# First stage of a transformer block: the w_ada sums on column groups of TensorE in place of VectorE

## The chip, the cores and the metric

The kernel runs on one core of one Trainium2 chip. The metric is the device time of one execution, in microseconds (us). Before the change three runs took 434.02 to 434.26 us, with a median of 434.11.

## The reference, cut to what matters

The block takes 256 tokens `x` of width 1024 and one conditioning vector `c`. Its first stage is this:

```
c_act = silu(c)
mod   = c_act @ w_ada + b_ada                  # 1024 x 6144; six parts of 1024
sh_m, sc_m, gt_m, sh_f, sc_f, gt_f = split(mod, 6)
h     = rms_norm(x, g_mix) * (1 + sc_m) + sh_m
proj  = h @ w_in                               # q, k, v of two attentions, and gates
```

Two attentions, a gated mix, and a feed-forward part with a short convolution follow; the change doesn't touch them. All inputs are fp32.

## The kernel before, in words

Each weight product is made of three fp32r products: a high part (`hh`, `wh`, a rounded copy made by ScalarE) and a low part (`hl`, `wl`, the difference): hh·wh, hl·wh and hh·wl.

The first stage is a loop (L510) over the eight row blocks j of w_in, which are also the eight column blocks of the normed and modulated `h`. It is emitted in a fixed order: every engine runs its instructions as they stand in the code. Step j has these parts:

- `products` (L403): 24 matmuls `pA` of 256 moving columns into four PSUM banks (q and k) and 6 matmuls `pV` of 512 columns (v).
- For step j+1, ahead of the products of j: two transposes of x (L390) into a bank `h`, and the sums of the shift and scale columns of block j+1, that is c_act times 1024 rows of w_ada for 128 columns of each. Part of the eight row blocks k is summed on VectorE: `ada_mac` (L383, L385) multiplies each block by its element of c and adds up in `acc`; the list `KV` sets how many. The rest goes to TensorE in `sums` (L396), where a 128x128 block of w_ada is stationary and one column of c moves. `acc_sums` (L401) adds up `acc` over the partitions with a column of ones.
- `w_hi` (L478): ScalarE makes `whA` (1024 wide) and `whB` (512). It stands ahead of `modulated` in the code.
- `modulated`: VectorE makes `ab` (two columns, L441 and L443), ScalarE makes `hf` from the transposed x (L445) and `hh` (L446).
- `h_lo` (L492) and `w_lo` (L486): `hl`, `wlA` on VectorE and `wlB` on GpSimd; from step 2 on `hl` is GpSimd's too.
- `load_on`: the loads of w_ada block j+3 and w_in block j+2, on SyncE's queue, three slots for each.

Ahead of the loop c is read and passed through silu, TensorE runs 24 warm-up matmuls (L115), and `norm1` (L315) forms each token tile's root mean square: a square with a running sum on ScalarE (`sq`), `ms` on VectorE, a power on GpSimd, and the scaling of the first 256 columns of x on VectorE (L320). The other 768 columns follow in step 0 (L516). GpSimd also builds a table of biases (`rrow`, `rdram`), which comes back as `toep`.

Of the kernel before, what the change touches and what calls it, by code (L numbers as in the profile page):

```python
# [53 lines left out]
def block_kernel(ctx: ExitStack, tc: tile.TileContext, x, c, w_ada, b_ada, g_mix, w_in, w_br_moba,  # L54
# [53 lines left out]
    nc.vector.tensor_mul(ca, ce, cps[:, :KT])  # L108

# [237 lines left out]
    toep = att.tile([P, NH, S], F32, tag="gb", name="toep")  # L347
# [3 lines left out]
    M = [8, 0, 0, 0, 0, 0, 0, 0]  # L351
    KV, KV0 = [4, 4, 5, 6, 7, 7, 7, 7], [5, 4]
# [16 lines left out]
    def win_load(j):
        raw = raw_tile(f"wA{j}")  # L370
        nc.sync.dma_start(raw[:, :1536], w_in[j * P:(j + 1) * P, QA:QA + 1536])
        return raw

    def kv(j, i):
        return KV0[i] if j == 0 else KV[j]

    def ada_mac(j, wk, acc=None, parts=slice(0, 2)):
        if acc is None:
            acc = small.tile([P, 2, P], F32, tag="acc0", name=f"acc0_{j}")
        a = acc[:, parts, :]  # L380
        for k in range(kv(j, parts.start)):
            if k == 0:
                nc.vector.tensor_scalar(a, wk[:, parts, 0, :], ca[:, 0:1], None, op0=ALU.mult)  # L383
            else:
                nc.vector.scalar_tensor_tensor(a, wk[:, parts, k, :], ca[:, k:k + 1], a, op0=ALU.mult, op1=ALU.add)  # L385
        return acc

    def transposes(j, ps, ts=range(NT)):
        for t in ts:
            nc.tensor.transpose(ps[:, t * P:(t + 1) * P], xs[t][:, j * P:(j + 1) * P], ident)  # L390

    def sums(j, ps, wk):

        for i in range(2):
            for k in range(kv(j, i), KT):
                nc.tensor.matmul(ps[:, S + i:S + i + 1], wk[:, i, k, :], ca[:, k:k + 1],  # L396
                                 start=i == 0 and k == kv(j, 0), stop=False)

    def acc_sums(j, ps, acc, parts=(0, 1)):
        for i in parts:  # L400
            nc.tensor.matmul(ps[:, S + i:S + i + 1], acc[:, i, :], ones[:, 0:1], start=False, stop=i == 1)  # L401
# [47 lines left out]
    wks = {0: ada_load(0)}  # L449
    vr = const.tile([108, P], F32, name="vr")  # L450
# [5 lines left out]
    wws = {0: win_load(0)}  # L456
    for j in (1, 2):
        wks[j] = ada_load(j)
    wws[1] = win_load(1)
    r1 = [norm1(0)]  # L460
    acc0 = ada_mac(0, wks[0], parts=slice(0, 1))
    r1.append(norm1(1))
    ada_mac(0, wks[0], acc0, slice(1, 2))
# [6 lines left out]
    gmix, gffn, bconv = vc[:, 48:56], vc[:, 56:64], vc[:, 64:108]  # L470

# [9 lines left out]
    def w_lo(j, wh):  # L481

        wl = wlp.tile([P, 1024], F32R, tag="wl", name=f"wlA{j}"), wlp.tile([P, 1024], F32R, tag="wl", name=f"wlB{j}")

        def piece(eng, i, a, n):
            eng.tensor_sub(wl[i][:, a:a + n], wws[j][:, i * 1024 + a:i * 1024 + a + n], wh[i][:, a:a + n].bitcast(F32))  # L486

        piece(nc.gpsimd, 1, 0, 512)
        return [(wh[i], wl[i]) for i in range(2)], [lambda: piece(nc.vector, 0, 0, 1024)]

    def h_lo(j, hf):
        (nc.gpsimd if j > 1 else nc.vector).tensor_sub(hl[:, j, :], hf, hh[:, j, :].bitcast(F32))  # L492

    def load_on(j):
        if j + 3 < KT:
            wks[j + 3] = ada_load(j + 3)
        if j + 2 < KT:
            wws[j + 2] = win_load(j + 2)

    ps = bank(sm, "h1_0")  # L500
    transposes(0, ps)
    sums(0, ps, wks[0])
    acc_sums(0, ps, acc0, (0,))
    acc_sums(0, ps, acc0, (1,))
    warm_up(8)
    wh = w_hi(0)
    next(wh)
    hf = modulated(0, ps)
    wh = list(wh)[-1]
    for j in range(KT):  # L510
        if j + 1 < KT:
            acc = ada_mac(j + 1, wks[j + 1])
        h_lo(j, hf)
        wp, fill = w_lo(j, wh)
        if j == 0:
            fill += [lambda t=t: nc.vector.tensor_scalar(xs[t][:, S:], xs[t][:, S:], r1[t], None, op0=ALU.mult)  # L516
                     for t in range(NT)]
        for f in fill:
            f()
# [270 lines left out]
    def pairs_put(p0):  # L790
        def put(t, ps):
            if p0 not in tb:
                tb[p0] = (att.tile([P, KT, S], F32R, tag="gb", name="qk01") if p0 == 0
                          else slot("h2h", [P, KT, S], F32R, "qk23"))
# [220 lines left out]
    wcr = [slot("trif", [88, P], F32, "wcr0"), slot("wcr1", [44, P], F32, "wcr1")]  # L1015
# [52 lines left out]
```

## Time and profile before

| | |
|---|---|
| median of three runs | 434.11 us |
| the profiled execution | 434.69 us, span 433.0 us |
| TensorE matmul / weight load busy | 410.1 us (95%) / 364.4 us (84%) |
| VectorE, ScalarE, GpSimd busy | 335.6 (77%), 254.0 (59%), 41.4 us (10%) |
| mean granted TensorE clock | 0.982 of full speed |
| moved by DMA | 94.44 MB, mean 218 GB/s |

The span is what the profiler saw from the first to the last instruction, and times in rows count from its start. A busy share is an average over stages of different kinds; the stage of the change is the first 67 us. In the timeline rows a piece begins at the first number and lasts the second; matmuls overlap in the pipeline, so the distance from one start to the next, not the duration, is what one costs in a row of many. An fp32 matmul shows as two instructions.

### The profile page before, as it was taken

To read this page: it belongs to the slowest core of one execution; us is meant where nothing else is said; L and a number is where in the kernel's file an instruction comes from. 1 tells how busy PE (TensorE), PEld (TensorE's weight loads), DVE (VectorE), ACT (ScalarE), POOL (GpSimd) and SP (SyncE) were. 2 spreads that over 40 slices of the span, in tenths; PEclk is the share of its full clock that TensorE was granted. 3 is DMA by queue.
4 is the path that set the end of the run, shared out by engine and by line. 5 is a ranking of instruction groups with operands and counts; after the bars stand their busy time and mean duration, and the time that the engine had idled before them with its cause. 6 is when DMAs were issued, how large, how long until landed. Compare 5 with 4: busy or idle time off the path is not lost.

```text
span 433.0 us, 6769 instructions
## 1 busy us (share of the span) xinstructions
PE 410.1 (95%) x2598; PEld 364.4 (84%) x2598; DVE 335.6 (77%) x509; ACT 254.0 (59%) x397; POOL 41.4 (10%) x76
## 2 busy tenths in 40 slices
PE   7899889999799899999996999999999999999993
PEld 7898887789698688788884899999999999888882
DVE  3789969689689977996858779999998888546333
ACT  3244537867966779942446758666776666433312
POOL 3624430000001010000041000000000000000001
PEclk9999969999999999999999999999999999999997
DMA  8999987988467556577537487677576655473102
GB/s 260 323 325 332 290 287 259 323 292 289 147 239 254 188 203 234 197 244 288 177 115 242 155 277 251 202 254 247 178 226 175 183 193 195 149 266 122 47 0 97
DMA packets 67128, 94.44 MB, mean 218 GB/s; under 512 B 2558, under 2 KB 45697, under 8 KB 67096
## 3 DMA queue, kind: packets, MB, share of 16 engines
q1 hardware_dynamic: 65943, 90.77, 63.6%
q0 software_dynamic: 576, 1.67, 1.2%
q10 hardware_dynamic: 576, 1.57, 1.0%
q8 instruction: 20, 0.33, 0.3%
q14 instruction: 13, 0.10, 0.1%
HBM read 92.94 MB, written 1.06 MB: 217 GB/s over the span
## 4 chain that ended last, share of the span: by engine, by line
PE 61%; DVE 13%; ACT 9%; DMA 8%; issue 4%; SPq 1%; POOL 1%; POOLq 0%; DVEq 0%; ACTq 0%
PE ps_up L252 26%; PE ps_down L164 14%; DVE acc L385 4%; PE ps_out L164 4%; DMA ada_gtm<-in_w_ada_dram 3%; PE ps_yb L164 3%; PE ps_ya L164 3%; PE ps_qkb L252 3%; DMA raw_wA<-in_w_in_dram 2%; PE ps_up L164 2%; DMA ada<-in_w_ada_dram 2%; PE pA L406 1%; DMA ada_shf<-in_w_ada_dram 1%; DVE wl_gate L139 1%; SPq L365 1%
## 5 line engine op out<-in xcount | busy, mean ns | idle before, releaser
L138 ACT CAST wh_up<-raw_up 128x1024 fp32r<-128x1024 f32 x44 | 46.1, 1050 | 27.7 <-PE ps_up L252 21.9
L252 PE MATMUL ps_up<-h2h__2313,wh_up 128*128 128x256 f32 x320 | 58.0, 283 | 0.0
L252 PE MATMUL ps_up<-h2h__2313,wl_up 128*128 128x256 f32 x320 | 57.9, 283 | 0.0
L139 DVE TENSOR_TENSOR wl_up<-raw_up,wh_up 128x1024 fp32r<-128x1024 f32 x42 | 51.1, 1220 | 8.5 <-ACT wh_up L138 8.3
L252 PE MATMUL ps_up<-h2l__2314,wh_up 128*128 128x256 f32 x320 | 57.1, 279 | 0.0
L252 PEld LDWEIGHTS ps_up<-h2h__2313,wl_up 128*128 128x128 f32 x320 | 46.9, 191 | 0.0
L139 DVE TENSOR_TENSOR wl_down<-raw_down,wh_down 128x1024 fp32r<-128x1024 f32 x22 | 26.9, 1224 | 25.6 <-ACT wh_down L138 25.6
L252 PEld LDWEIGHTS ps_up<-h2l__2314,wh_up 128*128 128x128 f32 x320 | 46.6, 190 | 0.0
L252 PEld LDWEIGHTS ps_up<-h2h__2313,wh_up 128*128 128x128 f32 x320 | 46.4, 189 | 0.2
L138 ACT CAST wh_down<-raw_down 128x1024 fp32r<-128x1024 f32 x22 | 23.2, 1053 | 32.2 <-PE ps_down L164 23.6
L941 DVE SCALAR_TENSOR_TENSOR cv<-ps_up,wc,cv 128x255 f32<-128x255 f32 (+1 forms) x80 | 34.4, 476 | 1.4 <-ACT cv L935 0.9
L164 PE MATMUL ps_down<-wl_down,hh_a 128*128 128x512 f32 x88 | 34.9, 397 | 0.0
L164 PE MATMUL ps_down<-wh_down,hh_a 128*128 128x512 f32 x88 | 34.7, 395 | 0.0
L164 PE MATMUL ps_down<-wh_down,hl_a 128*128 128x512 f32 x88 | 34.7, 394 | 0.0
L164 PE MATMUL ps_gate<-wh_gate,hh 128*128 128x512 f32 x64 | 26.2, 409 | 1.9 <-DVE vbl L145 1.5
L385 DVE SCALAR_TENSOR_TENSOR acc<-ada,ca,acc 128x256 f32<-128x256 f32 (+1 forms) x43 | 24.7, 576 | 1.5
L164 PE MATMUL ps_gate<-wl_gate,hh 128*128 128x512 f32 x64 | 25.4, 396 | 0.0
L164 PE MATMUL ps_gate<-wh_gate,hl 128*128 128x512 f32 x64 | 25.3, 396 | 0.0
L935 ACT ACTIVATE cv<-ps_up,vc,wc 128x256 f32<-128x256 f32 x40 | 20.5, 562 | 5.7 <-PE ps_up L252 5.7
L139 DVE TENSOR_TENSOR wl_gate<-raw_gate,wh_gate 128x1024 fp32r<-128x1024 f32 x16 | 20.3, 1286 | 3.2 <-ACT wh_gate L138 3.2
L478 ACT CAST whA<-raw_wA 128x1024 fp32r<-128x1024 f32 (+1 forms) x9 | 8.6, 958 | 22.9 <-DMA raw_wA<-in_w_in_dram 22.9
L164 PEld LDWEIGHTS ps_down<-wh_down,hh_a 128*128 128x128 f32 x88 | 16.5, 188 | 4.1
(268 smaller groups left out, 930.7 us busy)
## 6 DMA issues: line engine op xcount, KB each, us to landing
raw_up<-in_w_up_dram SPq DMA_DIRECT2D x44, 512.0 KB, 5.0
raw_down<-in_w_down_dram SPq DMA_DIRECT2D x10, 1024.0 KB, 5.0
ada<-in_w_ada_dram SPq DMA_DIRECT2D x16, 512.0 KB, 7.5
raw_gate<-in_w_in_dram SPq DMA_DIRECT2D x8, 1024.0 KB, 7.2
raw_wA<-in_w_in_dram SPq DMA_DIRECT2D x8, 768.0 KB, 9.0
raw_qkb<-in_w_in_dram SPq DMA_DIRECT2D x8, 512.0 KB, 5.7
ada_gtm<-in_w_ada_dram SPq DMA_DIRECT2D x8, 512.0 KB, 5.4
ada_shf<-in_w_ada_dram SPq DMA_DIRECT2D x8, 512.0 KB, 5.7
```

The lines of the kernel that those rows point to most:

```text
L138: nc.scalar.copy(wh[:, :n], t[:, a:a + n])
L139: (lo or nc.vector).tensor_sub(wl[:, :n], t[:, a:a + n], wh[:, :n].bitcast(F32))
L164: nc.tensor.matmul(ps, sx(k)[:, sl], w[:, c0:c0 + n], start=first and i == 0, stop=last and i == 2)
L252: nc.tensor.matmul(st.ps[f // 2][:, f % 2 * S:(f % 2 + 1) * S], wi[:, kk * 512 + f * P:kk * 512 + (f + 1) * P], sx(k0 + kk), start=first a ...
L365: nc.sync.dma_start(raw[:, i * D:(i + 1) * D].rearrange("p (k f) -> p k f", f=P), w_ada[:, i * D + j * P:i * D + (j + 1) * P].rearrange("( ...
L385: nc.vector.scalar_tensor_tensor(a, wk[:, parts, k, :], ca[:, k:k + 1], a, op0=ALU.mult, op1=ALU.add)
L406: nc.tensor.matmul(psqk[f // 2][:, f % 2 * S:(f % 2 + 1) * S], wp[0][n == 2][:, f * P:(f + 1) * P], (hh, hl, hh)[n][:, j, :], start=j == 0 ...
L478: nc.scalar.copy(wh[i][:, a:a + n], wws[j][:, i * 1024 + a:i * 1024 + a + n])
L935: nc.scalar.activation(ct[:, b, :], tp[:, b * S:(b + 1) * S], AF.Identity, bias=bconv[:, fb:fb + 1], scale=wc[:, 88 + fb:89 + fb])
L941: nc.vector.scalar_tensor_tensor(ct[:, b, d:], tp[:, b * S:(b + 1) * S - d], wc[:, (2 - d) * 44 + fb:(2 - d) * 44 + fb + 1], ct[:, b, d:], ...
```

## The change

Per step, all eight row blocks of the w_ada sums go to TensorE with the roles changed: a 128x32 tile `cw` with one column of c in its first column (the other 31 are zero) is stationary, and 256 columns of w_ada (128 of the shift, 128 of the scale) move. Block k writes to the 32 PSUM partitions that begin at 32·(k mod 4), so four column groups of the array are used, each twice. VectorE copies the 128x256 result to `row`, and two matmuls with a column of ones turn it into two columns. x is scaled in full and transposed ahead of the loop into a tile `xT`. `ab` goes from VectorE to ScalarE, `hl` and `wlB` from GpSimd to VectorE. w_ada has four slots of its own in a pool that is closed behind the stage, and two loads more are issued ahead of the loop.

```diff
+    cw = const.tile([P, KT, 32], F32, name="cw")
+    nc.vector.memset(cw, 0.0)
+    nc.vector.tensor_copy(cw[:, :, 0], ca)
...
     def norm1(t):
         sq = slot(f"xn{t}", [P, D], F32, f"sq{t}")
         ss = small.tile([P, 1], F32, tag="ss1", name=f"ss1_{t}")
         nc.scalar.activation(sq, xs[t], AF.Square, accum_out=ss)
         r = rstd_of(ss, f"n1_{t}")
-        nc.vector.tensor_scalar(xs[t][:, :S], xs[t][:, :S], r, None, op0=ALU.mult)
-        return r
+        for half in range(2):
+            sl = slice(half * 512, (half + 1) * 512)
+            nc.vector.tensor_scalar(xs[t][:, sl], xs[t][:, sl], r, None, op0=ALU.mult)
+        for half in range(2):
+            tp = bank(sm, f"xt{t}{half}")
+            for a in range(4):
+                j = 4 * half + a
+                nc.tensor.transpose(tp[:, a * P:(a + 1) * P], xs[t][:, j * P:(j + 1) * P], ident)
+            nc.scalar.copy(xT[:, 4 * half:4 * half + 4, t * P:(t + 1) * P], tp.rearrange("p (a b) -> p a b", a=4))
...
-    M = [8, 0, 0, 0, 0, 0, 0, 0]
-    KV, KV0 = [4, 4, 5, 6, 7, 7, 7, 7], [5, 4]
+    M1, M2 = 4, 12
...
+    def row_sums(j):
+        cs = bank(sm, f"cs_{j}")
+        for k in range(KT):
+            g = slice(k % 4 * 32, k % 4 * 32 + 32)
+            nc.tensor.matmul(cs[g, 0:S].rearrange("p (i f) -> p i f", i=2), cw[:, k, :], ads[j][:, :, k, :],
+                             start=k < 4, stop=k >= 4)
+        row = small.tile([P, S], F32, tag="acc0", name=f"row_{j}")
+        nc.vector.tensor_copy(row, cs[:, 0:S])
+        return row
+
+    def column_sums(j, row):
+        ps = bank(sm, f"h1_{j}")
         for i in range(2):
+            nc.tensor.matmul(ps[:, i:i + 1], row[:, i * P:(i + 1) * P], ones[:, 0:1], start=i == 0, stop=i == 1)
+        return ps
...
     def modulated(j, ps):
-        nc.vector.tensor_scalar(ab[:, 0:1], ps[:, S + 1:S + 2], b1[:, 8 + j:9 + j], gmix[:, j:j + 1],
-                                op0=ALU.add, op1=ALU.mult)
-        nc.vector.tensor_scalar(ab[:, 1:2], ps[:, S:S + 1], vc[:, j:j + 1], None, op0=ALU.add)
+        nc.scalar.activation(ab[:, 0:1], ps[:, 1:2], AF.Identity, bias=bg[:, j:j + 1], scale=gmix[:, j:j + 1])
+        nc.scalar.activation(ab[:, 1:2], ps[:, 0:1], AF.Identity, bias=vc[:, j:j + 1])
-        nc.scalar.activation(hf, ps[:, :S], AF.Identity, bias=ab[:, 1:2], scale=ab[:, 0:1])
+        nc.scalar.activation(hf, xT[:, j, :], AF.Identity, bias=ab[:, 1:2], scale=ab[:, 0:1])
...
     for j in range(KT):
         todo = products(j, wp)
         if j + 1 < KT:
-            run(todo, M[j])
-            transposes(j + 1, ps)
-            sums(j + 1, ps, wks[j + 1])
-            acc_sums(j + 1, ps, acc)
+            run(todo, M1)
+            row = row_sums(j + 1)
+            run(todo, M2)
+            hf = modulated(j + 1, column_sums(j + 1, row))
+            h_lo(j + 1, hf)
             wh = list(w_hi(j + 1))[-1]
-            hf = modulated(j + 1, ps)
+            wp = w_lo(j + 1, wh)
         run(todo)
```

TensorE before, where the products of step 2 have ended; `h_4` is the bank of block 4, `ada` its part of w_ada, `pA` the q and k banks with the products of step 3, `pV` those of v:

```order
L390 MATMUL h_4_486<-ident,x_94 128x128
L390 MATMUL h_4_486<-ident,x_96 128x128
L396 MATMUL h_4_486<-ca,ada_402 128x1 x2
L401 MATMUL h_4_486<-ones,acc_4_473 128x1 x2
L406 MATMUL pA_146<-hh,whA_428 128x256 x2
L406 MATMUL pA_147<-hh,whA_428 128x256 x2
L406 MATMUL pA_148<-hh,whA_428 128x256 x2
L406 MATMUL pA_149<-hh,whA_428 128x256 x2
L411 MATMUL pV_150<-whB_429,hh 128x512
```

TensorE now, at the start of the products of step 3; `cs` is the bank of the row sums of block 4:

```order
L405 MATMUL pA_150<-hh,whA_469 128x256 x2
L405 MATMUL pA_151<-hh,whA_469 128x256 x2
L390 MATMUL cs_500<-ada_363,cw 32x256 x8
L405 MATMUL pA_152<-hh,whA_469 128x256 x2
L405 MATMUL pA_153<-hh,whA_469 128x256 x2
L410 MATMUL pV_154<-whB_470,hh 128x512
L410 MATMUL pV_155<-whB_470,hh 128x512
L405 MATMUL pA_150<-hl,whA_469 128x256 x2
L405 MATMUL pA_151<-hl,whA_469 128x256 x2
L405 MATMUL pA_152<-hl,whA_469 128x256 x2
L399 MATMUL h_4_523<-ones,row_509 128x1 x2
L405 MATMUL pA_153<-hl,whA_469 128x256 x2
```

The transposes and one-column matmuls that stood between two steps are gone; the row sums stand behind four products of step 3, and the column sums (`h_4`) come 12 products later, with 14 behind them.

ScalarE before, from the squares of x to the first step's casts:

```order
L318 ACTIVATE sq_172,ss_0_173<-x_94 128x1024
L318 ACTIVATE sq_186,ss_1_187<-x_96 128x1024
L467 COPY vc<-vps 128x108
L478 CAST whA_259<-raw_wA_162 128x512
L445 ACTIVATE hf_265<-h_0_239,ab_262 128x256
L446 CAST hh<-hf_265 128x256
L478 CAST whA_259<-raw_wA_162 128x512
L478 CAST whB_260<-raw_wA_162 128x512
```

ScalarE now, the same place; `xt` are banks of transposed x:

```order
L326 ACTIVATE sq_181,ss_0_182<-x_95 128x1024
L336 COPY xT<-xt_190 128x4x128
L336 COPY xT<-xt_196 128x4x128
L326 ACTIVATE sq_202,ss_1_203<-x_97 128x1024
L336 COPY xT<-xt_211 128x4x128
L336 COPY xT<-xt_217 128x4x128
L464 COPY vc<-vps 128x108
L440 ACTIVATE ab_284<-h_0_281,bg,vc 128x1
L441 ACTIVATE ab_284<-h_0_281,vc 128x1
L443 ACTIVATE hf_287<-xT,ab_284 128x256
L444 CAST hh<-hf_287 128x256
```

The square of the second token tile (`sq`) stood right behind the first; now two copies out of the transposes' banks stand between them, and four copies ahead of `ab` and `hf` of step 0.

ScalarE before, for step 3 in the loop:

```order
L478 CAST whA_428<-raw_wA_405 128x1024
L478 CAST whB_429<-raw_wA_405 128x512
L445 ACTIVATE hf_435<-h_3_419,ab_432 128x256
L446 CAST hh<-hf_435 128x256
```

ScalarE now, for step 3:

```order
L440 ACTIVATE ab_462<-h_3_459,bg,vc 128x1
L441 ACTIVATE ab_462<-h_3_459,vc 128x1
L443 ACTIVATE hf_465<-xT,ab_462 128x256
L444 CAST hh<-hf_465 128x256
L477 CAST whA_469<-raw_wA_366 128x1024
L477 CAST whB_470<-raw_wA_366 128x512
```

The casts `whA` and `whB` stood ahead of `hf` and `hh`; now they stand behind them, and the two `ab` ahead.

## Rows read from the trace of the kernel before

**Rows 1.** Stretches: length, busy PE, PEld, DVE, ACT, POOL (count); clock, DMA share, GB/s

```profile
20.00:50.00 30.00, 28.49 (x213) 26.58 (x212) 28.23 (x51) 12.61 (x22) 12.62 (x10) 1.00 1.11 334
...
56.00:62.00 6.00, 6.00 (x25) 5.61 (x26) 5.06 (x6) 2.87 (x4) 2.05 (x3) 0.50 0.82 252
```

**Rows 2.** DMA issues to 56 us: count, KB each, median us to landing

```profile
ada<-in_w_ada_dram SPq DMA_DIRECT2D x16, 512.0 KB, 7.5
raw_wA<-in_w_in_dram SPq DMA_DIRECT2D x8, 768.0 KB, 9.0
```

**Rows 3.** Timeline of ScalarE: start, length, line, operation, count, idle before and its releaser

```profile
4.19 1.06 ACT L318 ACTIVATE sq<-x 128x1024 f32<-128x1024 f32 x1 [0.98 <-DMA x<-in_x_dram]
...
14.19 0.41 ACT L446 CAST hh<-hf 128x256 fp32r<-128x256 f32 x1
...
14.50 0.61 ACT L478 CAST whA<-raw_wA 128x512 fp32r<-128x512 f32 x1
...
22.53 1.05 ACT L478 CAST whA<-raw_wA 128x1024 fp32r<-128x1024 f32 x1 [6.89 <-DMA raw_wA<-in_w_in_dram]
...
24.00 0.56 ACT L445 ACTIVATE hf<-h,ab 128x256 f32<-128x256 f32 x1
```

**Rows 4.** Timeline of TensorE's matmuls in the first stage

```profile
10.53 0.26 PE L465 MATMUL vps<-ident,vr 108*128 108x108 f32 x1
...
14.70 1.22 PE L406 MATMUL pA<-hh,whA 128*128 128x256 f32 x8
...
41.94 0.61 PE L401 MATMUL h<-ones,acc 128*128 128x1 f32 x4 [0.40 <-DVE acc L385]
...
42.40 1.19 PE L406 MATMUL pA<-hh,whA 128*128 128x256 f32 x8
...
43.90 1.10 PE L406 MATMUL pA<-hl,whA 128*128 128x256 f32 x8
...
46.73 0.38 PE L390 MATMUL h<-ident,x 128*128 128x128 f32 x2
...
46.94 0.50 PE L396 MATMUL h<-ca,ada 128*128 128x1 f32 x4
...
55.54 1.01 PE L401 MATMUL h<-ones,acc 128*128 128x1 f32 x4 [1.64 <-DVE acc L385]
...
56.41 2.05 PE L406 MATMUL pA<-hh,whA 128*128 128x256 f32 x8
...
63.41 0.40 PE L406 MATMUL pA<-hh,whA 128*128 128x256 f32 x2
```

**Rows 5.** Timeline of TensorE around an fp32 matmul of 512 columns

```profile
110.41 1.02 PE L725 MATMUL bc_gtm<-acc_gtm,ones 128*128 128x512 f32 x2
110.86 0.80 PE L252 MATMUL ps_qkb<-hh,wh_qkb 128*128 128x256 f32 x2
111.50 0.40 PE L252 MATMUL ps_qkb<-hh,wl_qkb 128*128 128x256 f32 x2
```

**Rows 6.** First two matmuls on 64 rows: ns min/median/max, first and last start

```profile
L592 PE MATMUL s<-ka,qa x2: 382/383/384, 67.7 to 67.7; 64*128 64x256 f32 x2
```

**Rows 7.** Timeline of TensorE around twelve matmuls on 64 rows

```profile
80.79 0.90 PE L592 MATMUL s<-ka,qa 64*128 64x256 f32 x12
81.62 0.50 PE L164 MATMUL ps_gate<-wh_gate,hh 128*128 128x512 f32 x1
```

**Rows 8.** A small ScalarE operation out of PSUM: ns min/median/max, start

```profile
L105 ACT ACTIVATE ce<-cps x1: 178/178/178, 3.0 to 3.0; 128x8 f32<-128x8 f32 x1
```

**Rows 9.** A 512-column ScalarE copy out of PSUM: ns min/median/max, first and last start

```profile
L728 ACT COPY gt_m<-bc_gtm x2: 592/598/603, 116.5 to 117.9; 128x512 f32<-128x512 f32 x2
```

**Rows 10.** Timeline of VectorE: the first `ms` and scaling

```profile
5.38 0.15 DVE L127 TENSOR_SCALAR ms_n<-ss 128x1 f32<-128x1 f32 x1 [1.53 <-ACT sq L318]
6.22 0.35 DVE L320 TENSOR_SCALAR x<-x,rstd_n 128x256 f32<-128x256 f32 x1 [0.69 <-POOL rstd_n L129]
```

**Rows 11.** Group of line, engine, operation: the later scaling: busy us, mean ns

```profile
L516 DVE TENSOR_SCALAR x<-x,rstd_n 128x768 f32<-128x768 f32 x2 | 1.1, 616 | 0.0
```

More of the change, by code (lines that the diff above doesn't have):

```diff
@@ L73, in block_kernel @@
     dram = ctx.enter_context(tc.tile_pool(name="dram", bufs=1, space=DRAM))
-    att_scope = ExitStack()
-    att = att_scope.enter_context(tc.tile_pool(name="att", bufs=1))
-    aw = att_scope.enter_context(tc.tile_pool(name="aw", bufs=1))
+    att_scope, st_scope = ExitStack(), ExitStack()
+    attb = att_scope.enter_context(tc.tile_pool(name="attb", bufs=1))
+    toep = attb.tile([P, NH, S], F32, tag="gb", name="toep")
+    st = st_scope.enter_context(tc.tile_pool(name="st", bufs=1))
     def bank(pool, name):
@@ L312, in columns @@
         return loader
+    xT = st.tile([P, KT, S], F32, name="xT")
     def norm1(t):
@@ L369, in win_load @@
     def win_load(j):
[L370 to L392, printed above, removed]
-        for i in range(2):
[L395 to L401, printed above, removed]
+        wws[j] = raw_tile(f"wA{j}")
@@ new lines, in win_load @@
+        nc.sync.dma_start(wws[j][:, :1536], w_in[j * P:(j + 1) * P, QA:QA + 1536])
+    def row_sums(j):
[7 more added lines that the diff above has]
+        return row
@@ L454, in block_kernel @@
     nc.sync.dma_start(rb, rel_bias)
-    wws = {0: win_load(0)}
+    win_load(0)
     for j in (1, 2):
[L458 to L463, printed above, removed]
+        ada_load(j)
+        win_load(j)
+    ada_load(3)
+    for t in range(NT):
+        norm1(t)
     vps = bank(sm, "vps")
@@ L470, in block_kernel @@
     gmix, gffn, bconv = vc[:, 48:56], vc[:, 56:64], vc[:, 64:108]
+    bg = const.tile([P, KT], F32, name="bg")
+    nc.vector.tensor_mul(bg, b1[:, 8:16], gmix)
     bias_rows()
@@ L483, in w_lo @@
         wl = wlp.tile([P, 1024], F32R, tag="wl", name=f"wlA{j}"), wlp.tile([P, 1024], F32R, tag="wl", name=f"wlB{j}")
[L485 to L489, printed above, removed]
+        for i, n in ((0, 1024), (1, 512)):
+            nc.vector.tensor_sub(wl[i][:, 0:n], wws[j][:, i * 1024:i * 1024 + n], wh[i][:, 0:n].bitcast(F32))
@@ L491, in h_lo @@
+        return [(wh[i], wl[i]) for i in range(2)]
     def h_lo(j, hf):
[L492 to L506, printed above, removed]
@@ L507, in block_kernel @@
-    next(wh)
-    hf = modulated(0, ps)
-    wh = list(wh)[-1]
-    for j in range(KT):
[L511 to L519, printed above, removed]
+        nc.vector.tensor_sub(hl[:, j, :], hf, hh[:, j, :].bitcast(F32))
@@ L520, in block_kernel @@
+    row = row_sums(0)
+    warm_up(4)
+    hf = modulated(0, column_sums(0, row))
+    warm_up(4)
+    wh = list(w_hi(0))[-1]
+    h_lo(0, hf)
+    wp = w_lo(0, wh)
+    for j in range(KT):
         todo = products(j, wp)
         if j + 1 < KT:
-            run(todo, M[j])
-            ps = bank(sm, f"h1_{j + 1}")
-            transposes(j + 1, ps)
-            sums(j + 1, ps, wks[j + 1])
-            acc_sums(j + 1, ps, acc)
+            run(todo, M1)
[3 more added lines that the diff above has]
+            h_lo(j + 1, hf)
@@ L534, in block_kernel @@
         tick()
+    st_scope.close()
+    att = att_scope.enter_context(tc.tile_pool(name="att", bufs=1, reuse_waits="tile"))
+    aw = att_scope.enter_context(tc.tile_pool(name="aw", bufs=1, reuse_waits="tile"))
     start.close()
@@ L792, in put @@
             if p0 not in tb:
[L793 removed]
+                tb[p0] = (attb.tile([P, KT, S], F32R, tag="gb", name="qk01") if p0 == 0
                           else slot("h2h", [P, KT, S], F32R, "qk23"))
```

24 lines of the change are left out of this document (11 added, 13 removed).

## Prediction

> **What bounds the kernel now.** I read the busy table by stretches first [rows 1]. From 20 to 50 us TensorE is busy 28.49 of 30 us, VectorE 28.23, and the DMA engines run full (share 1.11, 334 GB/s): three resources end almost together. The DMA issues [rows 2] say why: the stage needs 16 x 512 KB of w_ada and 8 x 768 KB of w_in, 14.7 MB, or with the 1 MB of x 15.7 MB, which at 334 GB/s is 47 us. ScalarE's cast of w_in row block 1 waits for its transfer (the row at 22.53) [rows 3].
>
> The end of the stage is not DMA's, though. The loop on TensorE [rows 4]: the products of step 4 begin at 42.40 and give way at 46.73 (4.33 us for 24 `pA` and 6 `pV` of twice their columns, so 4.33 / 36 = 0.12 us per 256 columns); the row sums of step 7 start at 55.54 after 1.64 us of waiting for VectorE's `acc`. Right behind that wait the clock goes to half (0.50 from 56 to 62 us [rows 1]), and the products of step 6, from 56.41 to 63.41, take 7.00 us instead of 4.33. Call T0 the start of the first products, 14.70, and T7 that of the last, 63.41 [rows 4]. What follows T7 is the same code before and after, so I forecast T7 and carry its shift to the end: the later stages keep TensorE fed from the same three weight slots, and nothing in their order changes.
>
> **What goes.** VectorE loses all `acc` multiply-adds and the two `ab` operations per step, GpSimd its `wlB` and `hl`. VectorE's new loop is one copy, `hl`, `wlA` and `wlB`, less than 3 us. TensorE loses the one-column matmuls over w_ada; the two transposes per step move ahead of the loop. VectorE can no longer end a step.
>
> **What comes, per step.** Eight fp32 matmuls of 256 moving columns. The nearest row of the price is the fp32 matmul of 512 columns [rows 5], which is two instructions: these and an ordinary pair run from 110.41 to 111.50, 1.09 us; less 0.24 for the pair, the two passes take 0.85 us, 0.43 each. At 256 columns a pass is 0.213 us, and there are 16 of them, because each of the eight matmuls is two instructions with the same columns of the array. One after another that is R = 3.41 us. Four at a time it is 4 x 0.213 = 0.85 us. Do separate parts of the array run together? The trace has it for halves of the rows [rows 6, 7]: the first two 64-row matmuls both last 382 to 384 ns inside one piece of 0.39 us, so they start together; but twelve of them take 0.83 us to the next matmul, where two at a time would need 3 x 0.12 + 3 x 0.06 = 0.54 (half of them have 128 columns), and one at a time 1.08. The overlap is real and about half of the ideal. In the new order the two passes of one matmul stand next to each other on the same 32 columns, so only the second pass of one group can lie beside the first pass of the next: 16 passes take 9 places, R = 9 x 0.213 = 1.92 us. I take 1.92 and keep 0.85 and 3.41 as ends.
>
> The change of array shape is priced by the row of two transposes at 46.73 [rows 4]: 0.38 us, of which the next matmul waits only until 46.94, leaves some 0.16 us of tail, which two changes per step could expose, 8 x 2 x 0.16 = 2.6 us in all; below nothing it can't go. I put nothing in the sum, since that tail lies beside the next matmul everywhere in the loop, and 2.6 in the range. The Trainium skill speaks against me there ("TensorEngine Tiling (Array Packing)", Key Properties): changing the tiling mode drains the engine, so by that rule the sum would be 2.6 us higher. No row here shows a change of column tiling.
>
> **The step in the loop.** The order on TensorE is 4 products, the row sums, 12 products, the column sums, 14 products. The next step's first product needs `hh` and the cast `whA`, and on ScalarE both now stand behind the column sums: `ab`, `ab`, `hf`, `hh`, `whA`. From one step's first product to the next: 16 products, 1.50 for ten (42.40 to 43.90) and six more at 0.12, 2.2 us; R; column sums 0.61 [rows 4]; a handing-on of 0.1 (the first `hh` ends at 14.60, its product begins at 14.70 [rows 3, 4]); two `ab` at 0.18, the nearest small ScalarE row [rows 8], 0.36; `hf` 0.56; `hh` 0.31 to the next start (14.19 to 14.50); `whA` 1.05 [rows 3]; 0.1. The sum is 5.29 + R. Behind the column sums only 14 products, 2.13 us, cover 2.48 us of this, so TensorE idles some 0.4 us per step, which before `whA` ahead of `hf` hid. VectorE's copy of the row sums waits for `wlB`, done about 2 us into the step, and is covered by the 12 products.
>
> **The start.** Before, x is scaled only in its first 256 columns and two transposes stand ahead of the first sums. Now all of x is scaled and transposed first, and on ScalarE the second `sq` stands behind two copies out of PSUM that need TensorE, which is behind its 24 warm-up matmuls until 10.53 [rows 4]. From there: four transposes 0.6; two copies 0.6 each [rows 9], 12.3; `sq` to `ms` 1.19 (4.19 to 5.38) and to the scaling 0.84 (5.38 to 6.22) [rows 3, 10], 14.35; two scalings of 512, between the 256 of that row and 0.62 for 768 [rows 11], 0.5 each, 15.4; the last transposes 0.6, 16.0. Then R, the copy 0.4, and the chain above with half a `whA` (0.61): 0.61 + 0.1 + 0.36 + 0.56 + 0.31 + 0.61 + 0.1 = 2.65. T0 = 19.05 + R, against 14.70. TensorE stands idle from about 11.5 to 15, longer than the 1.64 us behind which the clock fell before; a fall costs from nothing up to 3.1 us (7.00 - 4.33 and 0.4 on the sums). I take 1.0, since part of it lies in time when TensorE waits for ScalarE anyway.
>
> **Sum.** T7 = 19.05 + R + 7 x (5.29 + R) = 56.1 + 8R, to set against 63.41: 8R - 7.3. The change pays only below R = 0.91 us. With 1.92: +8.1, with the clock +9.1. The profiled execution took 434.69, so 443.8; the runs' median lies 0.58 below it, so 443.2. DMA doesn't end the stage: 15.7 MB and the 1 MB of `toep`, which GpSimd, free of its loop, now issues early, are 50 us of transfer. The step of some 7 us leaves them idle time; the transfers that come early cost nothing.
>
> **Rivals.**
> *Four groups at once.* R = 0.85 to 1.0. T7 = 56.1 + 6.8 = 62.9, -0.5; if the queue of `ab` to `whA` is also shorter than I add up, the step is bound by TensorE's own 4.33 + 0.85 + 0.61 = 5.79 instead of 6.14, and seven of them give 2.5 more. Time 431 to 435, middle 433. For it: the pair that starts together [rows 6]. Against: two passes per matmul on the same columns, and the late start. This is the case on the other side; it decides at R = 0.91. The Trainium skill ("TensorE: Matmul & The Clock Gate", Packing small matmuls) gives the span of a packed set as one matmul plus a few ns per tile, by which R is 0.85, but it also says that matmuls start and end in program order, by which it is my 1.92. The pair in the trace agrees with the overlap.
> *No overlap of the groups*, so that the change only moves VectorE's work onto TensorE: R = 3.41, T7 = 83.4, +20.0 and the clock 1.0, time 455. For it: nothing in the trace runs in column groups. Against: the same pair.
> *The clock falls again in the loop.* With waits of 0.4 us per step and thinly filled row sums, three falls like that of 56 to 62 us cost 3 x 3.1: 443.2 + 9.3 = 452.5. For it: the fall behind 1.64 us. Against: 0.40 us before the sums at 41.94 [rows 4] was followed by none, at clock 1.00 [rows 1].
>
> **How the numbers follow.** Forecast 0.44, its own range 440 to 447 (drains, the handing-on, the clock at both ends). Four at once 0.28, no overlap 0.15, clock in the loop 0.10, 0.03 for what I don't see. Leaving out most of the no-overlap case above and a little below, the range is 431.5 to 453.5. A measurement can tell 0.2%, 0.9 us, from no change. Of four at once 0.17 lies below 433.2 and 0.11 within; 0.04 of faster comes from the low edges of the others: faster 0.21, same 0.11, slower 0.68.
>
> **What would show it.** The start of the first `pA` near 21 us; from first product to first product 7.2 us, with `whA` ending last; the eight `cs` matmuls from first to the next `pA` start in 1.9 us, not 0.9 or 3.4; no VectorE release ahead of TensorE in the loop; the last products from about 72 us. If the `cs` block takes under 1 us the forecast is wrong, and if T0 stays below 17 us its other half.

## The result and the profile after

The changed kernel takes 440.88 us (median of 4 runs, 438.80 to 442.09), the kernel before 434.19 us (four runs). The ratio is 1.0147 with a 95% interval of 1.0106 to 1.0189, so the change makes the kernel slower by 1.1 to 1.9%. The profiled execution of the changed kernel is the fastest of the four: 438.8 us, span 437.1 us, which is 4.1 us more than before.

Busy time by stretches, the same columns as [rows 1]:

```profile
13.00:14.00 1.00, 0.00 (x0) 0.00 (x0) 0.64 (x2) 0.00 (x0) 0.93 (x3) 0.50 1.15 296
18.00:19.00 1.00, 1.00 (x8) 0.93 (x5) 0.42 (x1) 0.00 (x0) 0.70 (x3) 0.50 1.22 292
...
20.00:50.00 30.00, 27.19 (x229) 21.40 (x231) 12.30 (x19) 15.38 (x33) 1.04 (x2) 1.00 1.12 332
50.00:60.00 10.00, 9.61 (x84) 7.70 (x76) 3.66 (x6) 3.69 (x9) 0.46 (x1) 1.00 0.50 165
```

From 20 to 50 us VectorE's busy time fell from 28.23 to 12.30 us and GpSimd's from 12.62 to 1.04 [rows 1]: what the change set out to remove is gone, and no step of the loop begins with a wait for VectorE any more. TensorE's own time is not the whole answer either: it is busy for 27.19 of 30 us, less than before. The clock stands at half from 13 to 19 us, ahead of the loop, and at 1.00 all through it. From 50 to 60 us the DMA engines are half idle.

TensorE's matmuls, the same columns as [rows 4]: the start, the first two steps, and the end of the stage.

```profile
9.74 1.04 PE L335 MATMUL xt<-ident,x 128*128 128x128 f32 x8
14.13 1.97 PE L335 MATMUL xt<-ident,x 128*128 128x128 f32 x8 [3.35 <-DVE x L330]
...
16.21 1.94 PE L390 MATMUL cs<-ada,cw 128*32 128x256 f32 x16
18.07 1.96 PE L121 MATMUL warm<-ident,ones 128*128 128x128 f32 x8
19.87 0.50 PE L399 MATMUL h<-ones,row 128*128 128x1 f32 x4
...
22.61 0.74 PE L405 MATMUL pA<-hh,whA 128*128 128x256 f32 x4 [1.24 <-ACT whA L477]
23.28 1.07 PE L390 MATMUL cs<-ada,cw 128*32 128x256 f32 x16
24.28 0.74 PE L405 MATMUL pA<-hh,whA 128*128 128x256 f32 x4
...
26.03 0.50 PE L399 MATMUL h<-ones,row 128*128 128x1 f32 x4
...
29.15 0.74 PE L405 MATMUL pA<-hh,whA 128*128 128x256 f32 x4 [0.40 <-ACT whA L477]
...
68.38 0.51 PE L405 MATMUL pA<-hh,whA 128*128 128x256 f32 x2 [0.39 <-ACT whA L477]
...
69.64 0.51 PE L405 MATMUL pA<-hh,wlA 128*128 128x256 f32 x2 [0.52 <-DVE wlA L483]
...
74.84 0.50 PE L170 MATMUL ps_gate<-wh_gate,hh 128*128 128x512 f32 x1 [0.87 <-DVE ka L151]
```

Three things are to be read here. The row sums of a step, 16 passes, run from 23.28 to 24.28: R = 1.00 us. From first product to first product is 6.54 us (22.61 to 29.15, and the same in the six steps after it), and each step begins with 0.39 to 0.40 us of waiting for ScalarE's `whA`. And the first step starts at 22.61 instead of 14.70 [rows 4], behind 3.35 us of idle time and the half clock.

The view of the tile `cs` in the same step of the changed kernel gives its 16 passes: count, minimum, median and maximum in ns, first and last start in us. The first line has those that start before 23.35 us, the second those before 23.60, the third all.

```profile
L390 PE MATMUL cs<-ada,cw x4: 403/403/403, 23.3 to 23.3; 128*32 128x256 f32 x4
L390 PE MATMUL cs<-ada,cw x8: 379/391/403, 23.3 to 23.5; 128*32 128x256 f32 x8
L390 PE MATMUL cs<-ada,cw x16: 379/379/403, 23.3 to 24.0; 128*32 128x256 f32 x16
```

The passes start in fours. By the single records of the trace the fours begin at 23.28, 23.52, 23.74 and 23.95 us. Within a four the starts lie 7 ns apart; from four to four it is 0.22 to 0.24 us, the time of about one pass (0.213 in the prediction). So four passes run beside each other, and the fours follow one another.

Behind the column sums of 26.03 the timeline of ScalarE in the changed kernel shows the other half of the step:

```profile
26.57 0.35 ACT L440 ACTIVATE ab<-h,bg,vc 128x1 f32<-128x1 f32 x1 [2.97 <-PE h L399]
26.82 0.25 ACT L441 ACTIVATE ab<-h,vc 128x1 f32<-128x1 f32 x1
27.11 0.60 ACT L443 ACTIVATE hf<-xT,ab 128x256 f32<-128x256 f32 x1
27.74 0.41 ACT L444 CAST hh<-hf 128x256 fp32r<-128x256 f32 x1
28.05 1.04 ACT L477 CAST whA<-raw_wA 128x1024 fp32r<-128x1024 f32 x1
```

ScalarE is idle for 2.97 us ahead of this chain and then works it off without a gap, until the next step's first product may begin at 29.15.

Part of the loss comes back later. The last products start 4.97 us later than before, `ps_gate` begins 6.4 us later, yet the end of the span is only 4.1 us later. Before, TensorE waited in the middle of the kernel for VectorE's `qk`, and the clock fell. The stretch from 116 to 120 us of the kernel before, columns as in [rows 1], shows it at 0.62:

```profile
116.00:120.00 4.00, 3.90 (x18) 3.61 (x19) 2.65 (x5) 3.45 (x5) 0.00 (x0) 0.62 0.01 4
```

And TensorE's timeline of the kernel before has the wait ahead of that stretch:

```profile
116.10 0.51 PE L252 MATMUL ps_qkb<-hh,wh_qkb 128*128 128x256 f32 x2 [2.39 <-DVE qk L148]
```

The changed kernel in the same stretch is at full clock (1.00). Its TensorE comes to that product later and waits less:

```profile
121.11 0.50 PE L258 MATMUL ps_qkb<-hh,wh_qkb 128*128 128x256 f32 x2 [1.06 <-DVE qk L154]
```

The wait of 2.39 us is 1.06 us after the change and the clock stays at 1.00. The lateness is 6.3 us at the first product `ps_qkb` (101.97 against 95.67), 3.5 us at the first `ps_vb` behind that place (135.89 against 132.43), and 4.1 at the end. I saw this in the traces only and made no experiment on it.

### The profile page after: what moved, and what is told of

The parts are those of the page before. It is cut to its first block, busy times and chain, and to the rows that moved or that the text cites. A ratio compares the mean times of both kernels' runs of the same rounds, so it can differ in the third digit from the quotient of the medians.

```text
span 437.1 us, 6855 instructions
## 1 busy us (share of the span) xinstructions
PE 410.2 (94%) x2660; PEld 356.5 (82%) x2660; DVE 313.5 (72%) x466; ACT 259.6 (59%) x417; POOL 23.3 (5%) x62
## 3 DMA queue, kind: packets, MB, share of 16 engines
HBM read 92.94 MB, written 1.06 MB: 215 GB/s over the span
## 4 chain that ended last, share of the span: by engine, by line
PE 62%; ACT 13%; DVE 10%; DMA 9%; issue 4%; POOL 1%; SPq 0%; POOLq 0%; DVEq 0%; ACTq 0%
PE ps_up L258 26%; PE ps_down L170 14%; PE ps_out L170 4%; PE pA L405 3%; DMA ada_shf<-in_w_ada_dram 3%; DMA ada<-in_w_ada_dram 3%; DMA ada_gtm<-in_w_ada_dram 3%; PE ps_ya L170 3%; PE ps_yb L170 3%; PE cs L390 2%; PE ps_up L170 2%; ACT whA L477 2%; DVE wl_gate L145 2%; ACT hf L443 1%; DVE acc_shf L684 1%
## 5 line engine op out<-in xcount | busy, mean ns | idle before, releaser
L919 ACT ACTIVATE cv<-ps_up,vc,wc 128x256 f32<-128x256 f32 x40 | 20.5, 562 | 5.6 <-PE ps_up L258 5.6
L487 DVE TENSOR_TENSOR hl<-hf,hh 128x256 fp32r<-128x256 f32 x8 | 3.4, 425 | 26.3 <-ACT hh L444 26.3
L145 DVE TENSOR_TENSOR wl_gate<-raw_gate,wh_gate 128x1024 fp32r<-128x1024 f32 x16 | 19.2, 1224 | 1.3 <-ACT wh_gate L144 1.3
L170 PEld LDWEIGHTS ps_down<-wh_down,hl_a 128*128 128x128 f32 x88 | 16.5, 188 | 3.9
```

What stands on the lines that cost most here:

```text
L145: (lo or nc.vector).tensor_sub(wl[:, :n], t[:, a:a + n], wh[:, :n].bitcast(F32))
L170: nc.tensor.matmul(ps, sx(k)[:, sl], w[:, c0:c0 + n], start=first and i == 0, stop=last and i == 2)
L487: nc.vector.tensor_sub(hl[:, j, :], hf, hh[:, j, :].bitcast(F32))
L919: nc.scalar.activation(ct[:, b, :], tp[:, b * S:(b + 1) * S], AF.Identity, bias=bconv[:, fb:fb + 1], scale=wc[:, 88 + fb:89 + fb])
```

## The experiments

**The changed kernel again**, without an edit, as the base of the others.

> The changed kernel unaltered, for the same chip as the others. The four runs so far lie between 438.8 and 442.1. My reading: the first stage is fixed (first products at 22.6 us, a step of 6.54 us, the last products 5 us later than before), and what varies is whether the clock falls once more where TensorE waits at the start of the qkb products (near 120 us; before it did, after 2.39 us of waiting; in the profiled run of the changed kernel, after 1.06 us, it did not). Theory: median 440 to 441. Rival (the first stage itself varies, by its own clock): the first products start elsewhere than at 22.6 us.

440.12 us (438.48 to 441.25), ratio 1.0127 [1.0098, 1.0156]. Its profiled execution (441.25, span 439.5) has the same step of 6.54 us, but everything begins later:

```profile
11.85 1.04 PE L335 MATMUL xt<-ident,x 128*128 128x128 f32 x8
...
23.70 0.74 PE L405 MATMUL pA<-hh,whA 128*128 128x256 f32 x4 [1.24 <-ACT whA L477]
```

The first transposes moved from 9.74 to 11.85 us and the first products from 22.61 to 23.70. The first stage's start differs by up to 2 us between two executions of the kernel, so starts are compared below from a point inside the stage too. The start is only part of the 2.4 us between the two spans: 1.1 are there at the first products, and 1.3 come behind 120 us. In this execution the clock fell twice where the first profile has 1.00, to a mean of 0.91 from 140 to 160 us and the same from 240 to 260:

```profile
140.00:160.00 20.00, 18.06 (x90) 14.14 (x89) 17.97 (x19) 14.91 (x21) 2.82 (x4) 0.91 0.52 188
```

The fall at the start is not the same either. Behind the same 3.35 us of idle time the clock is at 0.50 from 17 to 19 us only, and from the row sums to the first product it is 5.54 us (18.16 to 23.70) instead of 6.40 (16.21 to 22.61).

**No column groups**: `cw` is 128 columns wide and every row-sum matmul uses the whole array, so that the passes can't run beside each other. The result is the same sum.

```diff
-    cw = const.tile([P, KT, 32], F32, name="cw")
+    cw = st.tile([P, KT, P], F32, name="cw")
...
-            g = slice(k % 4 * 32, k % 4 * 32 + 32)
-            nc.tensor.matmul(cs[g, 0:S]..., start=k < 4, stop=k >= 4)
+            nc.tensor.matmul(cs[:, 0:S]..., start=k == 0, stop=k == KT - 1)
```

> The row sums go to the whole array: cw is 128 wide (one column of c, 127 of zeros), all eight row blocks add up on the same columns, so no column groups. Theory (the groups run four at a time, which is why the 16 passes took 1.00 us): without them 16 passes of 0.213 us, R = 3.4 us, eight times 2.4 us more, time 458 to 461. Rival (the passes are short for another reason, such as only 32 stationary columns to load): R stays near 1 us, time near 441.

461.1 us in one run. One step on TensorE:

```profile
25.94 0.75 PE L404 MATMUL pA<-hh,whA 128*128 128x256 f32 x4 [1.24 <-ACT whA L476]
26.52 3.62 PE L389 MATMUL cs<-ada,cw 128*128 128x256 f32 x16
29.79 0.82 PE L404 MATMUL pA<-hh,whA 128*128 128x256 f32 x4
...
34.74 0.74 PE L404 MATMUL pA<-hh,whA 128*128 128x256 f32 x4 [0.39 <-ACT whA L476]
```

The 16 passes take 3.27 us (26.52 to 29.79) instead of 1.00, and the step 8.80 instead of 6.54: 8.80 - 3.27 = 5.53, and 6.54 - 1.00 = 5.54. The rest of the step is 5.54 us for both values of R, and the row sums on four groups are 3.3 times as fast. The edit also makes each load of `cw` longer (a median of 190 ns for 128 columns, 106 to 110 for 32), so by itself it can't tell the groups from the shorter loads, the rival that I had named. The starts in fours 0.22 us apart, above, are what shows that the four groups run together.

**The order of the groups**: row blocks 2g and 2g + 1 go to group g, so that all four passes of a group stand next to each other.

```diff
-            g = slice(k % 4 * 32, k % 4 * 32 + 32)
+            g = slice(k // 2 * 32, k // 2 * 32 + 32)
...
-                              start=k < 4, stop=k >= 4)
+                              start=k % 2 == 0, stop=k % 2 == 1)
```

> Row blocks 0 and 1 go to column group 0, 2 and 3 to group 1 and so on, so that four passes on the same columns stand next to each other; the sums are the same. Theory of my forecast (passes start in program order, and a pass waits for the one ahead on its columns): only every fourth pass can lie beside its neighbour, 13 places of 0.213 us, R = 2.8 us against 1.00, time about 454. Rival (each column group takes its passes from a queue of its own, whatever the order): R stays at 1.0 us, time 438 to 442.

439.95 us in one run, and the row sums:

```profile
22.61 1.09 PE L390 MATMUL cs<-ada,cw 128*32 128x256 f32 x16
```

1.09 us against 1.07 with the groups taken in turn. The passes still start in fours, and the fours 0.22 to 0.24 us apart. Within a four the starts now lie 13 ns apart instead of 7, as they would if each four had one pass of every group; the trace doesn't name the group of a pass. My forecast's reason for R = 1.92, that neighbours on the same columns hold up the rest of the queue, fell: even four passes in a row on one group don't hold up the next group's.

**Casts first**: the next weights' casts stand ahead of `ab`, `hf` and `hh` on ScalarE, in the idle time before the column sums.

```diff
-            hf = modulated(j + 1, column_sums(j + 1, row))
-            h_lo(j + 1, hf)
+            hs = column_sums(j + 1, row)
             wh = list(w_hi(j + 1))[-1]
+            hf = modulated(j + 1, hs)
+            h_lo(j + 1, hf)
```

> The casts whA and whB of the next step are put ahead of ab, hf and hh on ScalarE, as before the change; nothing else moves. Theory (the chain behind the column sums sets the step, whA last): the step falls from 6.54 to TensorE's own work, about 4.33 + 1.0 + 0.5 = 5.9 us, seven steps are 4.4 us shorter, time 436 to 437. Rival (the step is set by the transfers of 1.8 MB per step, 5.5 to 5.7 us, or by VectorE): the step stays above 6.4 and the time at 440 to 441.

435.91 us (434.34 to 437.66), ratio 1.0037 [1.0018, 1.0056]. The row sums of neighbouring steps stand at 22.60, 28.47 and 34.33, so a step takes 5.86 to 5.87 us, and the wait for `whA` at the start of a step is gone:

```profile
27.91 0.63 PE L405 MATMUL pA<-hh,whA 128*128 128x256 f32 x4
...
33.77 0.63 PE L405 MATMUL pA<-hh,whA 128*128 128x256 f32 x4
```

**Column sums earlier** reaches the same end in another way: the order on ScalarE stays, but its chain starts six products sooner.

```diff
-    M1, M2 = 4, 12
+    M1, M2 = 4, 6
```

> The changed kernel with only the place of the column sums in the loop moved forward (M1, M2 = 4, 6), so that ScalarE's chain behind them starts earlier beside the hh products; casts and squares stay in their order. If the step is 6.54 us because ScalarE's chain of about 3.1 us behind the column sums ends last, the 0.4 us of TensorE's wait in each step goes, the step is 5.9 to 6.1 us and the time 436 to 438 us. Rival: the sums can't start earlier, since ada's squares or the weights' casts are what they wait for; then the step stays at 6.5 us and the time at 440 us.

436.24 us (434.37 to 437.24), ratio 1.0038 [1.0016, 1.0061]. TensorE in its second step:

```profile
29.64 0.64 PE L405 MATMUL pA<-hh,whA 128*128 128x256 f32 x4
30.20 1.07 PE L390 MATMUL cs<-ada,cw 128*32 128x256 f32 x16
...
35.51 0.63 PE L405 MATMUL pA<-hh,whA 128*128 128x256 f32 x4
```

The step is 5.87 us, with no wait. That is 0.67 us less for a wait of 0.40: where TensorE waited (29.15 in the changed kernel), the two products ahead of it also showed their tail (28.13 to 28.75 and then the wait, against 0.47 from 35.04 to 35.51 here), and the four behind it took 0.67 us instead of 0.56. Two different edits on the queue of `ab` to `whA` give the same step and the same time, 1.0037 and 1.0038 of the kernel before where the changed kernel had 1.0127. That is some 4 us, and the queue behind the column sums cost it.

**Warm-ups in the idle time**: 14 warm-up rounds between the first transposes and the second, to keep the clock up; nothing else.

```diff
+        if t == 0:
+            warm_up(14)
```

> 14 more warm-up matmuls (28 instructions, 3.0 us) stand between the transposes of the two token tiles, where TensorE was idle for 3.35 us. Theory (that idle time makes the clock fall to 0.50 from 13 to 19 us, and the transposes, row sums and warm-ups at half clock cost some 2 us): clock at 1.00 there, first products at 20.5 to 21 us instead of 22.6 to 23.7, time about 438.5. Rival (ScalarE's chain ends last there whatever the clock): first products unchanged, time 440.

440.50 us (439.96 to 443.56), ratio 1.0141 [1.0107, 1.0176]. The start on TensorE:

```profile
17.25 1.07 PE L390 MATMUL cs<-ada,cw 128*32 128x256 f32 x16
...
21.99 0.74 PE L405 MATMUL pA<-hh,whA 128*128 128x256 f32 x4 [1.24 <-ACT whA L479]
```

The first row sums take 1.07 us instead of 1.94, and from them to the first product it is 4.74 us, where the changed kernel's two profiles have 6.40 and 5.54: the half clock cost 1.66 and 0.80 us at that place. But the first products start at 21.99, not at 20.5 to 21 (the first transposes began at 11.54 us here, at 9.74 in the first profile), and the time is the rival's, not 438.5. In this profile the clock fell twice later in the kernel:

```profile
140.00:160.00 20.00, 17.70 (x87) 13.87 (x87) 18.00 (x21) 13.54 (x20) 1.77 (x3) 0.91 0.60 220
240.00:260.00 20.00, 17.74 (x85) 13.97 (x84) 15.88 (x27) 12.60 (x22) 1.54 (x2) 0.91 0.57 188
```

The changed kernel's first profile stood at 1.00 in both, but its second had 0.91 in both as well, so these falls come without the added warm-ups too. What the half clock costs is shown in the stage and not in the time.

**Both squares first**: the two `sq` and scalings stand ahead of all 16 transposes, so that ScalarE's second square no longer waits behind copies that need TensorE. (The loop over the transposes moved out of `norm1` into `turn1`.)

```diff
+    def turn1(t):
         for half in range(2):
             tp = bank(sm, f"xt{t}{half}")
...
+    for t in range(NT):
+        turn1(t)
     vps = bank(sm, "vps")
```

> The two squares of x stand together again on ScalarE and the two scalings on VectorE, and all 16 transposes follow; the loop is untouched. Theory (the late start is the queue of the second square behind the copies, and the clock that falls in the 3.35 us of idle time behind the first transposes): first products at 16 to 17 us instead of 22.6, the clock stays up, and all of the 6 us reach the end: 434 to 435. Rival (transfers pace the loop, so an early start is waited away): first products at 16 to 17, but the last products still near 66 to 68 us and the time at 439 to 441.

435.73 us (434.38 to 437.13), ratio 1.0023 [1.0005, 1.0042]. The 16 transposes begin at 10.43 and the row sums at 12.69, at full clock; the first product begins at 17.42, 5.2 us before the changed kernel's. One step in the loop, whose length is otherwise still 6.54 us, now loses 1.00 us more:

```profile
30.50 0.74 PE L407 MATMUL pA<-hh,whA 128*128 128x256 f32 x4 [0.39 <-ACT whA L481]
...
38.05 0.74 PE L407 MATMUL pA<-hh,whA 128*128 128x256 f32 x4 [1.39 <-ACT whA L481]
```

There `whA` itself waits 0.91 us for its transfer. The start is worth some 4.4 us of the median (440.12 less 435.73), not all of the 6 that I expected to reach the end, and behind it the transfers appear.

**Start and casts together.**

> The two edits of before together: casts ahead of the chain in the loop, and both squares ahead of the transposes. If they add up without a third limit, first products at 17.4 us, seven steps of 5.87, last products at 58.5 us: ten us less than in the changed kernel, time about 430. Theory now: transfers become the limit, since the cast of step 3 already waited 1.4 us for w_in with the early start alone; first products of step 3 near 38, then 5.6 to 5.9 per step, last products at 61 to 62, time 432 to 433. Rival (the later stages take back whatever the first gives): time 435 to 436, as either edit alone.

438.37 us (437.57 to 440.28), ratio 1.0110 [1.0081, 1.0139]. I expected 432 to 433. TensorE in the loop of this kernel:

```profile
31.29 1.07 PE L392 MATMUL cs<-ada,cw 128*32 128x256 f32 x16 [2.32 <-DMA ada<-in_w_ada_dram]
...
40.12 1.22 PE L407 MATMUL pA<-hh,whA 128*128 128x256 f32 x4 [3.36 <-ACT hh L446]
41.27 1.94 PE L392 MATMUL cs<-ada,cw 128*32 128x256 f32 x16
```

And the stretch from 40 to 60 us of the same kernel, columns as in [rows 1], where the clock averages 0.92:

```profile
40.00:60.00 20.00, 19.88 (x162) 15.96 (x166) 8.87 (x14) 10.96 (x23) 0.54 (x1) 0.92 0.90 283
```

And ScalarE, where the cast `whA` now stands ahead of `hh`:

```profile
37.03 1.04 ACT L481 CAST whA<-raw_wA 128x1024 fp32r<-128x1024 f32 x1 [9.12 <-DMA raw_wA<-in_w_in_dram]
```

With 6 us less start and steps of 5.87 us the weights don't all come in time. TensorE waits 2.32 us for `ada`; later `whA` waits for its transfer and holds `hh`, and with it TensorE, up for 3.36 us; then the clock stands at 0.50 from 40 to 43 us, and the next row sums take 1.94 us. Two gains of 4 us each add up to less than either.

**toep behind the weights**: as the last one, but `toep`'s load of 1 MB, which GpSimd issued at 20.1 us there (23.9 in the changed kernel, 55.1 before), is issued by SyncE behind the last `w_in`, at 44.9 us.

```diff
-        nc.gpsimd.dma_start(toep, bass.AP(...
+        nc.sync.dma_start(toep, bass.AP(...
```

> As the two edits together, and the 1 MB load of toep goes from GpSimd's queue to SyncE's, behind the last w_in load of the stage. Theory (1 MB of toep stands ahead of w_in block 3 since GpSimd has no loop left, 1 MB at 334 GB/s is 3.1 us): no wait of the cast of step 3, last products at 58 to 59, 2 to 3 us below the kernel with the two edits, if the gate loads behind toep still land in time: 429 to 431. Rival (toep's place doesn't matter): same as the two edits.

434.77 us (434.30 to 437.03), ratio 1.0023 [1.0005, 1.0042], 3.6 us below the one above, but not the 429 to 431 us that I expected. The long waits are gone; two short ones for `hh` remain, the second at the last step. ScalarE there:

```profile
57.85 2.00 ACT L144 CAST wh_gate<-raw_gate 128x1024 fp32r<-128x1024 f32 x2 [2.37 <-DMA raw_gate<-in_w_in_dram]
59.76 0.34 ACT L442 ACTIVATE ab<-h,bg,vc 128x1 f32<-128x1 f32 x1
```

Casts of the next stage's weights stand ahead of the last `ab`, wait 2.37 us for a transfer, and make `hh` late; the clock averages 0.76 from 60 to 66 us. So casts moved forward bring such waits into the queue ahead of `ab`. With the column sums moved forward the casts stay behind `hh`.

**toep's place alone**, in the changed kernel.

> The changed kernel with only toep's load moved from GpSimd's queue to SyncE's, behind the last w_in load. The forecast put the early transfer at nothing, because ScalarE's chain sets the step: then the first step's start and the steps of 6.54 us stay, and the time is 439.5 to 441 us. Rival: toep's 1 MB takes DMA time from ada and w_in in steps that wait for them; then the time is 436 to 438 us.

441.60 us (439.18 to 441.77), ratio 1.0141 [1.0104, 1.0177], against 1.0127 for the changed kernel: no gain. Every step still begins with 0.39 to 0.40 us of waiting for `whA`. At 6.54 us per step the transfers are not what ends it.

**Start, earlier column sums, and toep behind the weights**: the version that the others point to. **The same with toep on GpSimd's queue** as in the changed kernel.

> The start with both squares together, the column sums earlier in the loop (M2 = 6) and toep's load issued by SyncE behind the last w_in load. If start, ScalarE's chain and toep's place are the three things that made the change slower, the first step starts at about 17.5 us, steps take 5.9 us with one or two waits of 1 to 2 us for transfers, the last products of the stage begin at 59 to 61 us without a fall of the clock, and the time is 430 to 432.5 us. Rival: transfers set the end of the stage whatever the engines do; TensorE then waits 3 us or more in the loop, the clock falls, and the time is 434 to 435.5 us, no better than before.

> The start with both squares together and the column sums earlier (M2 = 6), but toep's load on GpSimd's queue as in the changed kernel. If its 1 MB counts once the steps are short, TensorE waits some 2 to 3 us more for ada or w_in in the loop than with the load behind the last w_in, and the time is 434.5 to 436.5 us. Rival: the place of that load is worth nothing here, and the time is 432 to 433.5 us.

With toep behind the weights: 432.71 us (429.86 to 433.93, 12 runs), ratio to the kernel before 0.9945 [0.9923, 0.9968]. It is 0.3 to 0.8% faster than the kernel before, so faster than both kernels, though 0.2 us above the range that I expected. Between the first step and the last, TensorE has no wait:

```profile
18.01 0.73 PE L407 MATMUL pA<-hh,whA 128*128 128x256 f32 x4 [1.24 <-ACT whA L481]
...
59.55 0.40 PE L407 MATMUL pA<-hh,whA 128*128 128x256 f32 x2
```

The last products start 3.86 us before those of before [rows 4] and 8.83 before the changed kernel's. With toep early, the loop has two waits:

```profile
31.11 1.07 PE L392 MATMUL cs<-ada,cw 128*32 128x256 f32 x16 [0.98 <-DMA ada<-in_w_ada_dram]
...
37.95 0.74 PE L407 MATMUL pA<-hh,whA 128*128 128x256 f32 x4 [1.36 <-ACT whA L481]
```

Its time is 433.72 us, ratio 0.9965 [0.9942, 0.9988]. The two intervals overlap: the 2.34 us of waits are in the trace, a difference in time between the two places is not shown, and the 434.5 us or more that I expected were not reached.

## Why the prediction was right on the side and wrong in its terms

Forecast 443.2, measured 440.88: slower, as forecast. That the sum came within 2.3 us is luck, because errors of both signs met in it. By its own steps:

| step of the forecast | forecast, us | measured, us |
|---|---|---|
| row sums R | 1.92 | 1.00 |
| step without R | 5.29 | 5.54 |
| first product T0 (19.05 + R, clock 1.0) | 22.0 | 22.61 |
| last products T7, clock included | 72.5 | 68.38 |
| shift carried to the end | +9.1 | +4.97 at T7, +4.1 at the end |

From the forecast's 72.46 (56.1 + 8 x 1.92 + 1.0): R takes off 8 x 0.92 = 7.36; seven steps add 7 x 0.25 = 1.75; the start adds 22.61 - 21.05 (19.05 + 1.00 + 1.0) = 1.56. That is 68.41, and 68.38 was measured.

**The step that failed is R.** I wrote that with two passes of a matmul next to each other on the same columns, "only the second pass of one group can lie beside the first pass of the next". The view of the 16 passes shows them starting four at a time, and the experiment on the order of groups shows that neighbours on the same columns hold nothing up. R = 1.00 lies at the upper end of the rival "four groups at once", and at the mark of 1 us that I had set for being wrong.

I had also misread the rows on half-array matmuls [rows 7], from which I took half of the ideal overlap. By the single records of that trace all twelve start in pairs, 3 to 4 ns apart within a pair. Most of the time beyond the ideal 0.54 us lies behind the first pair (0.23 us to the next one) and behind the last (0.20 us to the next matmul).

The price for changing the shape of the array was rightly left out of the sum: 4 x 0.213 = 0.85 us is the bare work of four groups, so both changes and everything else in the block cost some 0.15 us, where 0.32 would have been 2.6 us in all. Outside the block the step is as long as without column groups (5.54 and 5.53 us). The Trainium skill ("TensorEngine Tiling (Array Packing)", Key Properties) says that changing the tiling mode drains the engine. In this trace no drain beyond those 0.15 us shows. The Trainium skill ("TensorE: Matmul & The Clock Gate", Packing small matmuls) also says that a packed set takes one matmul and a few ns per tile. The fours in the trace, with starts 7 ns apart, agree with it.

**The rival with the right R had the wrong time.** It gave 431 to 435 us, because it supposed with me that T0 = 19.05 + R and that TensorE might set the step. Both failed:

*The step* was right in its mechanism. I named ScalarE's queue `ab`, `ab`, `hf`, `hh`, `whA` behind the column sums and 0.4 us of TensorE's idle time; both are in the rows, and from the column sums to the next product I had 3.09 us (2.48 and 0.61), measured 3.12. Both edits on this queue took 0.67 us off the step and some 4 us off the time. Of the 0.25 us by which my 5.29 fell short, 0.19 lie ahead of it: the four products before the row sums take 0.67 us instead of 4 x 0.12.

*The start* was the mis-sized term. Idle time of TensorE and a fall of the clock were forecast, at 1.0 us of a possible 3.1. With R = 1.00 my chain gives 20.05 without the fall; 22.61 came, 2.56 later. The row sums at half clock take 1.86 us instead of 1.00 (16.21 to 18.07), and behind them eight warm-up instructions (four matmuls) stand in the same queue, most of them also at half clock, so that the column sums begin at 19.87, though VectorE's copy of the row sums ended at 18.6:

```profile
18.21 0.42 DVE L393 COPY row<-cs 128x256 f32<-128x256 f32 x1 [0.92 <-PE cs L390]
```

I had counted no warm-up there. With the added warm-ups as the measure, 1.66 of the 2.56 us are the clock. Another 0.69 remain at full clock: 4.74 us from the row sums to the first product, where my chain has 4.05 (1.00, 0.4 and 2.65). The warm-ups that I hadn't counted are most of that. The last 0.21 lie ahead of the row sums (16.21, where I had 16.0). In the second profile the clock's part is 0.80 instead of 1.66. The order that makes the idle time cost some 4.4 us of the time.

**What was right**: VectorE no longer ends a step; the clock did not fall in the loop behind waits of 0.4 us (1.00 from 20 to 60 us), so that rival did not come; transfers that come early cost the changed kernel nothing, as toep's place alone shows. That last sentence holds only for a step of 6.54 us: with steps of 5.87 us and a start at 16.5 the same load was among the transfers that TensorE waited for.

**What I did not see**: the last step's `wlA` (0.52 us) and `ka` (0.87 instead of 0.35) with the tails around them, make the shift 6.4 us at `ps_gate`. By `ps_vb`, behind the shorter wait for `qk` and at full clock, 2.9 us of it are back, so "carried to the end" was too simple. The profiled execution was the fastest of its four, and the difference between its +4.1 and the medians' +6.7 is of the size that the second profile shows: 1.1 us in the start and 1.3 behind 120 us. What makes executions differ was not tried.

## What to carry to other kernels

When work moves off an engine that waits, follow the new chain through the queue of every engine that it passes, and start it as early as its inputs allow: here six products of head start were worth as much as a new order. Look at the start of a stage for itself: an idle stretch that the engine's clock answers is paid by everything that stands behind it, and warm-ups in the same queue can be part of the bill. Two gains measured apart need not add up; the next limit, here the transfers, has to be moved with them.

## What the runs showed of the hardware that I had not expected

- Sixteen fp32 passes of 128 rows, 32 columns and 256 moving columns took 1.00 us on four column groups, four starting at a time; on the whole array, with 128 columns, they took 3.27 us. The order in which the groups were taken made 0.02 us of difference.
- Behind TensorE's idle time of 3.35 us at the start the granted clock was 0.50 from 13 to 19 us in one execution and from 17 to 19 us in another of the same kernel; with warm-ups in that time it stayed at 1.00. Waits of 0.40 us in each step brought no fall.
